# Splits and set loads of a Strassen-Winograd step pipeline moved between engines, stages and queues

## The chip, the cores and the metric

The kernel runs on one core of a Trainium2 chip. The metric is device microseconds of one execution; a time that is given as the kernel's is the median of several. The engines are TensorE (PE), VectorE (DVE), ScalarE (ACT), GpSimd (POOL) and SyncE (SP), which only issues DMAs here. Each engine works through its own instructions in order.

## What is computed

One pre-norm decoder layer on 1024 tokens and 16 meta tokens, model width 1024, MLP width 4096, all in float32:

```python
h = rms_norm(x, norm1_w)
(rq, rk, rv, rg, dq, dk, dv, cb, cc, cx, gates) = [h @ w_in[:, s:e] for s, e in column_bounds()]
ret  = head_layer_norm(retention(rq, rk, rv)) * silu(rg)
diff = diff_attention(dq, dk, dv, lam, subln_w, lam_init)
conv = cb * short_conv(cc * cx, conv_w)
g = sigmoid(gates)                                    # three gates per channel
merged = g[0] * (ret @ w_branch[0]) + g[1] * (diff @ w_branch[1]) + g[2] * (conv @ w_branch[2])
x = x + merged @ w_out
u = square(relu(rms_norm(x, norm2_w) @ w_up))
return rms_norm(x + u @ w_down, final_norm_w)         # meta tokens dropped
```

## The kernel before

**Products in two parts.** Each float32 operand of a large product is held as a high part (a rounding copy, made by ScalarE, sometimes VectorE) and a low part (operand minus high part, a subtraction on VectorE or GpSimd). A product is three matmuls: high with high, high with low, low with high. `split` does both parts; `lo_part` the second alone, on the engine that `pick` takes in turn from a list.

**Mixers and gates stage.** Up to about 1085 us the input projections, attention, retention and convolution run, ordered by a planner. The three branch results lie in DRAM (`cT`, `dT`, `rT`). Then comes the gates stage: 24 groups of gate columns, 48 matmuls each. `weights` loads two halves of a weight tile and splits them, the low parts on GpSimd. From the third group on `branch_sums(br, k)` forms the right operands of the later products for one branch and one block row: it loads four blocks, makes the sums T1 to T4 on VectorE and stores these four (`TD`). It runs twelve times. At group 14 the first four operands of the first branch are loaded and split (`SET`).

**Steps.** From 1349 us on the order is written by hand (`tc.manual_schedule()`). All products (three branches, output projection, up, down) are a list of steps. A `Quad` makes two output pairs by seven products each (Strassen-Winograd, one level); step i is product i for both pairs, p = 0 and 1, 24 matmuls (12 in the half-height down block). The right operands are B11, B21, T1, B22, T2, T3, T4 in this order (`ORDER`), the left ones are weight blocks and their sums. In iteration s the loop issues, in this order:

```python
steps[s - 1][3](1)          # evac of pair 1 of the step before
soon ; steps[s + 2][1]()    # prep: weight sums, high and low parts of step s + 2
steps[s][2](0) ; mid ; steps[s][2](1) ; steps[s][3](0)     # 24 matmuls; evac of pair 0
work ; fetch                # splits of the next right operands; loads and stores
steps[s + 3][0]()           # weight loads of step s + 3
```

`Quad.pe` takes a bank for product 1 (kept and added to in products 5 to 7) and one for products 2, or 3 and 4; there are 8 banks (`acc_bank`). `Quad.evac` copies a bank out (L859) or calls `use`: in the branches L934 to L940 (add, times gate, plus the merged sum), in up L1116 to L1123 (square of relu), in down L1169 and L1170 (add the residual). Rings of buffers: 10 weight blocks (`raw`), 5 tiles of both parts (`w`), 3 gate blocks (`g`), 16 blocks (`X`).

**Right operands.** Two sets of 14 buffers hold the seven operands of a branch or down block in two parts. `turn_over` replaces them during the last quad: the block is loaded whole into the low half's buffer (L899) and split in place by `build`. Up's operands are made from the normalised output projection (`up_t1`, `plain_op`, `up_sum`): a scaling or a subtraction per block, then its parts. The quads of up begin with products 1 and 2 of two quads, as the others need the second half of the tokens, whose scale `token_scale(1)` makes in up's first step. `up_use` forms the sums for down and stores them (`UD`).

Of the kernel before, what the change touches and what calls it, by code (L numbers as in the profile page):

```python
# [18 lines left out]
P = 128  # L19
# [52 lines left out]
def trunk_kernel(ctx: ExitStack, tc, x, w_in, w_branch, w_out, w_up, w_down, w_down2, w_down3, vecs, lam_in, consts, y):  # L72
# [643 lines left out]
    TD = {br: {n: dram([P, 4, 512]) for n in ORDER if n not in PLAIN} for br, _ in BR}  # L716

    def right_src(br, name):
        if name in PLAIN:
            z, j = PLAIN[name]  # L720
            return dict(BR)[br][:, 4 * z:4 * z + 4, half(j)]
        return TD[br][name]
# [20 lines left out]
    for n, (br, f) in enumerate((br, f) for br, _ in BR for f in range(KT)):  # L743
        wt = weights(w_in[G_GATE + br * KT + f])
# [8 lines left out]
        if n == 14:  # L753

            SET = {}
            for name in ORDER[:4]:
                oh, ol = opnd(True, [P, 4, 512]), opnd(True, [P, 4, 512])
                nc.sync.dma_start(out=f32(ol), in_=right_src(2, name))
                for k in range(4):
                    split(f32(ol[:, k]), oh[:, k], ol[:, k], v if k % 2 else nc.gpsimd)  # L760
                SET[name] = (oh, ol)
# [22 lines left out]
    count = {}  # L784

    def pick(key, engines):
        count[key] = count.get(key, -1) + 1
        return engines[count[key] % len(engines)]

    G = nc.gpsimd  # L790

    def lo_part(key, engines, src, hi, lo):
        pick(key, engines).tensor_tensor(out=lo, in0=src, in1=f32(hi), op=ALU.subtract)  # L793

    class Quad:


        def __init__(self, srcs, nk, B, use, lo_engines, pre=False):
            self.srcs, self.nk, self.B, self.use, self.pre = srcs, nk, B, use, pre
            self.lo_engines = lo_engines  # L800
            self.A = [[None, None] for _ in range(7)]
            self.raw = {}
            self.kept = {}
# [71 lines left out]
    def new_set(first):  # L875
        return {}

# [8 lines left out]
    def build(src, oh, ol, key="set"):  # L886
        e = pick(key + "c", (a, a, a, v))
        if e is a:
            a.copy(out=oh, in_=src)  # L889
        else:  # L890
            v.tensor_copy(out=oh, in_=src)  # L891
        lo_part(key + "l", (v, v, v, G), src, oh, ol)

    def turn_over(L, B, nk, source, left_names):

        for i, name in enumerate(ORDER):
            def load(name=name):
                open_op(B, name, nk, name in left_names)
                nc.sync.dma_start(out=f32(B[name][1]), in_=source(name))  # L899

            def split_op(name=name):
                oh, ol = B[name]
                for k in range(nk):
                    build(f32(ol[:, k]), oh[:, k], ol[:, k])

            at(fetch, L + i + 1, load)
            at(work, L + i + 3, split_op)
# [10 lines left out]
    WLO = (G, G, G, v)  # L918
    SETS = {2: SET, 1: {}, 0: {}}
    for n, (br, _) in enumerate(BR):  # L920
        for quad in range(2):
# [8 lines left out]
            def use(p, r, j, pt, sb, br=br, quad=quad, gt=gt):  # L930
# [13 lines left out]
            q = Quad(pairs_of(w_branch[br * KT:(br + 1) * KT], quad), 4, SETS[br], use, WLO)  # L944
            for i in range(7):
                product_step(q, i)
        if n < 2:
            nxt = BR[n + 1][0]
            turn_over(L, SETS[nxt], 4, lambda name, nxt=nxt: right_src(nxt, name), FIRST)


    for i, name in enumerate(ORDER[4:]):
        def load(name=name):
            open_op(SET, name, 4, False)
            nc.sync.dma_start(out=f32(SET[name][1]), in_=right_src(2, name))

        def split_op(name=name):
            for k in range(4):
                build(f32(SET[name][1][:, k]), SET[name][0][:, k], SET[name][1][:, k])

        at(fetch, -1, load)
        at(work, 2 + i, split_op)
# [5 lines left out]
    def merged(f, js):  # L968
        if f not in MO:
            MO[f] = opnd(True, [P, 2, SEQ])  # L970
        for j in js:
            build(M[f, j], MO[f][:, 0, half(j)], MO[f][:, 1, half(j)])
# [13 lines left out]
    class Out:  # L986
# [13 lines left out]
        def prep(self):  # L1000
            for z in range(2):
                w = temp("w", [P, 2, 512], F32R)
                a.copy(out=w[:, 0], in_=self.raw[z])
                lo_part("o", (G, v), self.raw[z], w[:, 0], w[:, 1])
# [13 lines left out]
        def evac(self, p):  # L1018
# [8 lines left out]
            else:  # L1027
                sq[j] = temp("t", [P, 512])
                a.activation(out=sq[j], in_=xc, func=AF.Square)
                if f < KT - 1:  # L1030
                    G.tensor_tensor(out=acc[j], in0=acc[j], in1=sq[j], op=ALU.add)

        def store(self):
            nc.sync.dma_start(out=xd[:, self.f, half(self.j)], in_=X2[self.f, self.j])
# [27 lines left out]
    def up_op(name, k, src):  # L1062
        if k == 0:
            open_op(US, name, 4, name in U_LEFT)
        build(src, US[name][0][:, k], US[name][1][:, k], "up")
# [34 lines left out]
    UD = [{name: dram([P, n, 512]) for name in ORDER} for _, n in BLOCKS]  # L1100
# [4 lines left out]
    def up_use(pair):  # L1105
        U = {}

        def put(dst, src):
            at(fetch, now[0] + 1, lambda: nc.sync.dma_start(out=dst, in_=src))

        def store(name, src):
            for b, (p0, n) in enumerate(BLOCKS):
                if p0 <= pair < p0 + n:
                    put(UD[b][name][:, pair - p0, :], src)
# [226 lines left out]
```

## Time and profile before

| | |
|---|---|
| median of 3 runs | 2460.97 us (2460.46 to 2461.25) |
| profiled execution, its own time | 2457.13 us |
| its span | 2455.3 us |
| mean granted TensorE clock | 0.979 |

The profile is of one execution. Times in it are us from the start of the span. Matmuls are pipelined, so one is recorded at about 0.39 us while they follow each other every 0.23 us; what a stretch gets done is read from the count of its matmuls. "Granted clock" is the share of 2.4 GHz that TensorE got: 1.00, or 0.50 (1.2 GHz). A releaser behind "<-" is what ended the idle time or the wait before an instruction.

### The profile page before, as it was taken

The page shows a single profiled execution, that of the slowest core. Times are in us where ns is not written, and L with a number is a line of the kernel's source. Part 1 is how long each engine was busy: PE and PEld are TensorE (multiplying, and loading weights), DVE is VectorE, ACT ScalarE, POOL GpSimd, SP SyncE. Part 2 cuts the span into 40 slices and gives each one's busy share as a digit, 9 for nine tenths or more (in the row PEclk, how much of TensorE's full clock was granted, in tenths as well). Part 3 has the DMA queues.
Part 4 walks back from the last instruction along what each step waited for, and adds up shares of the span by engine and source line. Part 5 has one row for each costly group of instructions (what it writes and reads, how often), then busy time and mean ns, then how long its engine had stood idle before and what let it go on. Part 6 is the DMA issues. An engine that isn't in the chain of part 4 may idle for free. (4 is left out here: it accounts for less than half of the span.)

```text
span 2455.3 us, 32724 instructions
## 1 busy us (share of the span) xinstructions
PE 2330.6 (95%) x11854; PEld 2009.7 (82%) x11854; DVE 1570.2 (64%) x2963; ACT 987.6 (40%) x1929; POOL 918.4 (37%) x804
## 2 busy tenths in 40 slices
PE   7999999999999999999999888789979999999997
PEld 7999999999999989987887676567758888777766
DVE  6776776776764676565511576764676767665666
ACT  5554554554543333333322342323333334443344
POOL 2132223233222212126632345444534434555564
PEclk9999999999999999999999999899989999999999
DMA  3111111111111111129822453325425446544132
GB/s 135 35 52 44 44 52 44 44 52 44 44 53 44 52 52 52 52 99 346 315 99 96 145 179 132 138 95 183 148 75 166 154 146 234 199 152 161 67 130 70
DMA packets 123139, 271.48 MB, mean 111 GB/s; under 512 B 13920, under 2 KB 18144, under 8 KB 118752
## 3 DMA queue, kind: packets, MB, share of 16 engines
q1 hardware_dynamic: 111840, 231.63, 27.6%
q0 software_dynamic: 11136, 37.76, 3.9%
q8 instruction: 93, 1.52, 0.3%
q14 instruction: 70, 0.57, 0.1%
HBM read 195.41 MB, written 73.92 MB: 110 GB/s over the span
## 5 line engine op out<-in xcount | busy, mean ns | idle before, releaser
L161 PE MATMUL pmm<-H,whi 128*128 128x512 f32 (+3 forms) x1640 | 574.3, 352 | 14.2 <-ACT H L196 8.5
L162 PE MATMUL pmm<-H,whi 128*128 128x512 f32 (+3 forms) x1640 | 574.0, 351 | 1.6 <-DVE H L197 1.5
L163 PE MATMUL pmm<-H,wlo 128*128 128x512 f32 (+3 forms) x1640 | 572.9, 350 | 0.0
L850 PE MATMUL pb<-op,w 128*128 128x512 f32 x1176 | 480.1, 408 | 89.0 <-DVE t L934 31.7
L136 POOL TENSOR_TENSOR wlo<-raw,whi 128x512 fp32r<-128x512 f32 x190 | 256.7, 1352 | 638.1 <-ACT whi L135 590.1
L793 POOL TENSOR_TENSOR w<-raw,w 128x512 fp32r<-128x512 f32 (+1 forms) x248 | 347.9, 1411 | 361.7 <-ACT w L820 339.7
L852 PE MATMUL pb<-op,w 128*128 128x512 f32 x1176 | 473.3, 403 | 2.9 <-POOL w L793 2.8
L851 PE MATMUL pb<-op,w 128*128 128x512 f32 x1176 | 473.3, 402 | 1.2 <-POOL op L793 1.2
L820 ACT CAST w<-raw 128x512 fp32r<-128x512 f32 (+1 forms) x308 | 181.9, 601 | 502.7 <-DVE raw L826 218.8
L850 PEld LDWEIGHTS pb<-op,w 128*128 128x128 f32 x1176 | 228.6, 194 | 156.6 <-ACT t L859 36.7
L161 PEld LDWEIGHTS pmm<-H,whi 128*128 128x128 f32 x1640 | 309.2, 189 | 40.5 <-ACT H L196 8.5
L162 PEld LDWEIGHTS pmm<-H,whi 128*128 128x128 f32 x1640 | 309.9, 189 | 27.0 <-DVE H L197 2.3
L163 PEld LDWEIGHTS pmm<-H,wlo 128*128 128x128 f32 x1640 | 309.7, 189 | 24.4
L852 PEld LDWEIGHTS pb<-op,w 128*128 128x128 f32 x1176 | 228.3, 194 | 58.2 <-POOL w L793 5.1
L851 PEld LDWEIGHTS pb<-op,w 128*128 128x128 f32 x1176 | 229.0, 195 | 52.5 <-POOL op L793 1.5
L135 ACT CAST whi<-raw 128x512 fp32r<-128x512 f32 x192 | 118.6, 619 | 193.6 <-PE pmm L162 70.7
L793 DVE TENSOR_TENSOR w<-raw,w 128x512 fp32r<-128x512 f32 (+1 forms) x92 | 87.2, 948 | 138.7 <-ACT w L820 98.2
L826 DVE TENSOR_TENSOR raw<-raw,raw 128x512 f32<-128x512 f32 (+1 forms) x176 | 130.9, 771 | 59.3 <-DMA raw<-w_branch 38.2
L793 DVE TENSOR_TENSOR op<-op,op 128x512 fp32r<-128x512 f32 x114 | 101.4, 941 | 30.9 <-ACT op L889 30.9
L859 ACT COPY t<-pb 128x512 f32<-128x512 f32 x132 | 75.8, 582 | 44.1 <-PE pb L852 43.8
L378 ACT ACTIVATE B<-B,nb 128x144 f32<-128x144 f32 (+3 forms) x64 | 50.6, 791 | 99.3 <-DVE nb L377 99.0
L793 POOL TENSOR_TENSOR op<-op,op 128x512 fp32r<-128x512 f32 x38 | 56.2, 1480 | 88.9 <-DVE op L891 79.6
(285 smaller groups left out, 3874.9 us busy)
## 6 DMA issues: line engine op xcount, KB each, us to landing
raw<-w_in SPq DMA_DIRECT2D x192, 256.0 KB, 2.6
op<-d SPq DMA_DIRECT2D x42, 1024.0 KB, 7.6
d<-X SPq DMA_DIRECT2D x118, 256.0 KB, 3.1
raw<-w_up SPq DMA_DIRECT2D x72, 256.0 KB, 4.4
raw<-w_down SPq DMA_DIRECT2D x56, 256.0 KB, 3.5
d<-t POOLq DMA_DIRECT2D x48, 256.0 KB, 3.8
raw<-d SPq DMA_DIRECT2D x48, 256.0 KB, 7.4
d<-raw POOLq DMA_DIRECT2D x48, 256.0 KB, 6.7
```

Source lines behind the costliest of these rows:

```text
L135: a.copy(out=hi, in_=src)
L136: (eng or v).tensor_tensor(out=lo, in0=src, in1=f32(hi), op=ALU.subtract)
L161: nc.tensor.matmul(pt, lhsT=hi[:, s], rhs=xh[:, c0:c0 + w], start=start, stop=False)
L162: nc.tensor.matmul(pt, lhsT=hi[:, s], rhs=xl[:, c0:c0 + w], start=False, stop=False)
L163: nc.tensor.matmul(pt, lhsT=lo[:, s], rhs=xh[:, c0:c0 + w], start=False, stop=stop)
L793: pick(key, engines).tensor_tensor(out=lo, in0=src, in1=f32(hi), op=ALU.subtract)
L820: a.copy(out=w[:, 0], in_=src)
L826: comb = lambda d, x0, x1, o: v.tensor_tensor(out=d, in0=x0, in1=x1, op=o)
L850: nc.tensor.matmul(pt, lhsT=w[0][:, s], rhs=b[0][:, k], start=first, stop=False, skip_group_check=True)
L851: nc.tensor.matmul(pt, lhsT=w[0][:, s], rhs=b[1][:, k], start=False, stop=False, skip_group_check=True)
L852: nc.tensor.matmul(pt, lhsT=w[1][:, s], rhs=b[0][:, k], start=False, stop=k == nk - 1, skip_group_check=True)
L859: a.copy(out=t, in_=pt)
```

## The change

In the steps GpSimd makes no additions or subtractions any more: low parts, additions of the merged sum, of the squares and of the residual all run on VectorE, high parts all on ScalarE. In the gates stage the weights' low parts go to VectorE too. `branch_sums` splits five of the seven operands (B11, B21, T1, B22, T2) and stores both parts; T3 and T4 stay whole. Set loads, the stores of the residual and of up's results go from SyncE's queue to GpSimd's. In up, B11 and B21 for down are split before they are stored; the sums of the second pair come a step later; relu and square run on ScalarE alone. Three quads of up, not two, lead with their first two products. In an iteration `work` comes before the evacuation of pair 0, and the weight loads before `fetch`.

```diff
+    READY = ORDER[:5]
+    TD = {br: {n: dram([P, 2, 4, 512] if n in READY else [P, 4, 512]) for n in ORDER} for br, _ in BR}
+    def ready(br, k, n, src):
+        w = temp("w", [P, 2, 512], F32R)
+        split(src, w[:, 0], w[:, 1])
+        nc.gpsimd.dma_start(out=TD[br][n][:, :, k], in_=f32(w))
...
+        for n, zj in PLAIN.items():
+            ready(br, k, n, b[zj])
...
-        for n, t in (("T1", t1), ("T3", t3), ("T2", t2), ("T4", t4)):
+        for n, t in (("T3", t3), ("T4", t4)):
             nc.gpsimd.dma_start(out=TD[br][n][:, k], in_=t)
+        ready(br, k, "T1", t1)
+        ready(br, k, "T2", t2)
...
-        wt = weights(w_in[G_GATE + br * KT + f])
+        wt = weights(w_in[G_GATE + br * KT + f], lo_eng=v)
...
-                oh, ol = opnd(True, [P, 4, 512]), opnd(True, [P, 4, 512])
-                nc.sync.dma_start(out=f32(ol), in_=right_src(2, name))
-                for k in range(4):
-                    split(f32(ol[:, k]), oh[:, k], ol[:, k], v if k % 2 else nc.gpsimd)
+                SET[name] = [opnd(True, [P, 4, 512]) for _ in range(2)]
+                for z in range(2):
+                    nc.sync.dma_start(out=f32(SET[name][z]), in_=TD[2][name][:, z])
...
-            a.copy(out=w[:, 0], in_=src)
-            lo_part("w", self.lo_engines, src, w[:, 0], w[:, 1])
+            split(src, w[:, 0], w[:, 1])
...
+    def turn_over(L, B, nk, source, in_parts, left_names):
+        def load(name, z):
+            if z == 0:
+                open_op(B, name, nk, name in left_names)
+            G.dma_start(out=f32(B[name][z]), in_=source(name)[:, z])
...
+            if name in in_parts:
+                for z in range(2):
+                    at(fetch, L + i + 1 + z, lambda name=name, z=z: load(name, z))
+            else:
+                at(fetch, L + i + 1, lambda name=name: whole_load(name))
+                whole += [(name, k) for k in range(nk)]
...
+        n0 = 7 - len(whole) // nk
+        for n, (name, k) in enumerate(whole):
+            at(work, L + n0 + 3 + n // 3 * (1 if nk == 4 else 2), lambda name=name, k=k: split_op(name, k))
...
-                    pick("m", (G, v)).tensor_tensor(out=M[f, j], in0=M[f, j], in1=g, op=ALU.add)
+                    v.tensor_tensor(out=M[f, j], in0=M[f, j], in1=g, op=ALU.add)
...
+    U_READY = ("B11", "B21")
+    UD = [{name: dram([P, 2, n, 512] if name in U_READY else [P, n, 512]) for name in ORDER} for _, n in BLOCKS]
...
-            if sb is None:
-                a.activation(out=u, in_=pt, func=AF.Relu)
-                a.activation(out=u, in_=u, func=AF.Square)
-            else:
+            if sb is not None:
                 v.tensor_tensor(out=u, in0=pt, in1=sb, op=ALU.add)
-                v.scalar_tensor_tensor(out=u, in0=u, scalar=0.0, in1=u, op0=ALU.max, op1=ALU.mult)
+            a.activation(out=u, in_=pt if sb is None else u, func=AF.Relu)
+            a.activation(out=u, in_=u, func=AF.Square)
...
-                at(work, now[0] + 1, sums)
+                at(work, now[0] + 1 + p, sums)
...
+            for name in U_READY:
+                u, h = U[PLAIN[name]], temp("X", [P, 512])
+                split(u, h.bitcast(F32R), u.bitcast(F32R))
+                store(name, h, u)
...
-    for q, i in [(q, i) for q in range(2) for i in range(2)] + [(q, i) for q in range(2) for i in range(2, 7)] + \
-            [(q, i) for q in range(2, 8) for i in range(7)]:
+    for q, i in [(q, i) for q in range(3) for i in range(2)] + [(q, i) for q in range(3) for i in range(2, 7)] + \
+            [(q, i) for q in range(3, 8) for i in range(7)]:
...
-            pick("d", (G, v)).tensor_tensor(out=sb, in0=sb, in1=xc, op=ALU.add)
+            v.tensor_tensor(out=sb, in0=sb, in1=xc, op=ALU.add)
...
                 steps[s][2](1)
-                steps[s][3](0)
             for fn in work.get(s, ()):
                 fn()
+            if 0 <= s < N:
+                steps[s][3](0)
+            if 0 <= s + LL < N:
+                steps[s + LL][0]()
             for fn in fetch.get(s, ()):
                 fn()
-            if 0 <= s + LL < N:
-                steps[s + LL][0]()
```

The same edits are made in the output projection (`Out.prep`, `Out.evac`, `Out.store`), in `up_op`, `merged`, `last_u`, `last_w` and in the loads of the first branch's T2, T3 and T4.

## Rows read from the trace of the kernel before

**Rows 1.** The page, part 1: busy us, share of the span, instructions.

```profile
PE 2330.6 (95%) x11854; PEld 2009.7 (82%) x11854; DVE 1570.2 (64%) x2963; ACT 987.6 (40%) x1929; POOL 918.4 (37%) x804
```

**Rows 2.** Windows: length, busy us (instructions) per engine, granted clock, DMA share, GB/s.

```profile
1097.00:1217.00 120.00, 118.48 (x511) 95.59 (x511) 68.72 (x78) 35.75 (x62) 75.72 (x99) 1.00 0.95 339
1217.00:1349.00 132.00, 131.75 (x571) 106.75 (x569) 18.92 (x25) 28.96 (x47) 43.79 (x49) 1.00 0.30 99
1349.00:1655.00 306.00, 255.93 (x1010) 201.29 (x1011) 206.90 (x245) 99.37 (x179) 142.87 (x96) 0.92 0.40 139
1655.00:1748.00 93.00, 90.42 (x387) 72.88 (x386) 47.12 (x58) 34.36 (x59) 43.49 (x32) 0.98 0.55 176
1748.00:1826.00 78.00, 57.49 (x204) 42.94 (x203) 58.73 (x79) 25.65 (x44) 29.98 (x21) 0.87 0.26 89
1826.00:2085.00 259.00, 259.00 (x1123) 211.44 (x1123) 177.77 (x219) 99.78 (x171) 103.84 (x72) 0.99 0.52 171
2085.00:2348.00 263.00, 245.29 (x1035) 196.53 (x1034) 167.01 (x223) 102.99 (x188) 145.84 (x105) 0.98 0.42 153
2348.00:2381.00 33.00, 28.18 (x116) 21.11 (x115) 23.71 (x40) 15.40 (x36) 21.72 (x21) 1.00 0.25 80
```

**Rows 3.** Waits of PE from 1349 to 2381: us in total, times, longest.

```profile
PE pb L850 <- DVE t L934: 31.7, 7, 5.3
PE pb L850 <- ACT t L859: 29.5, 12, 6.3
PE pb L850 <- DVE X L1170: 16.6, 8, 4.0
...
PE pb L1047 <- ACT t L1029: 0.2, 1, 0.2
```

**Rows 4.** Windows of one wait in the branches and the matmuls behind it.

```profile
1388.30:1392.90 4.60, 0.24 (x2) 0.00 (x0) 4.56 (x6) 0.99 (x2) 2.94 (x2) 0.90 0.18 57
1393.00:1398.60 5.60, 5.60 (x13) 4.40 (x14) 2.04 (x4) 0.62 (x1) 0.62 (x1) 0.50 0.56 185
```

**Rows 5.** Timeline of DVE: start, us, instruction, count merged.

```profile
1156.76 0.69 DVE L735 TENSOR_TENSOR raw<-raw,raw 128x512 f32<-128x512 f32 x1
...
1374.10 1.88 DVE L793 TENSOR_TENSOR op<-op,op 128x512 fp32r<-128x512 f32 x3
...
1384.32 4.07 DVE L793 TENSOR_TENSOR op<-op,op 128x512 fp32r<-128x512 f32 x3
```

**Rows 6.** Timeline of POOL at the first and the last of these.

```profile
1157.02 0.56 POOL L738 DMA_DIRECT2D d<-raw  x1 [0.94 <-DVE raw L734]
...
1383.81 3.44 POOL L793 TENSOR_TENSOR w<-raw,w 128x512 fp32r<-128x512 f32 x2
```

**Rows 7.** Groups of POOL from 1349 to 2381, the costliest: count | busy, mean ns.

```profile
L793 POOL TENSOR_TENSOR w<-raw,w 128x512 fp32r<-128x512 f32 x223 | 325.6, 1468 | 353.9 <-ACT w L820 332.1 <-ACT w L1003 21.4
```

**Rows 8.** Waits of SP's DMA queue from 1349 to 1655.

```profile
SPq L928 <- POOL X L940: 143.1, 13, 18.5
```

**Rows 9.** Groups of ACT from 1349 to 2381, the costliest.

```profile
L820 ACT CAST w<-raw 128x512 fp32r<-128x512 f32 x276 | 168.6, 620 | 470.8 <-DVE raw L826 205.2 <-PE pb L852 129.3 <-DMA raw<-w_branch 72.4
```

**Rows 10.** Timeline of DVE in the start of up.

```profile
1756.48 0.69 DVE L192 SCALAR_TENSOR_TENSOR k<-t,k 128x512 f32<-128x512 f32 x1
...
1813.82 0.68 DVE L1082 TENSOR_TENSOR X<-X,X 128x512 f32<-128x512 f32 x1
1815.18 0.69 DVE L793 TENSOR_TENSOR op<-X,op 128x512 fp32r<-128x512 f32 x1 [0.69 <-ACT op L889]
1815.79 0.68 DVE L1082 TENSOR_TENSOR X<-X,X 128x512 f32<-128x512 f32 x1
```

**Rows 11.** Window in the branches with the densest set loads.

```profile
1431.00:1443.00 12.00, 7.18 (x29) 5.51 (x28) 8.37 (x12) 4.04 (x8) 5.78 (x5) 0.87 1.03 387
```

**Rows 12.** Timeline of PE at token scale, in up's first step.

```profile
1751.22 1.02 PE L1046 MATMUL pb<-k,onesr 128*128 128x512 f32 x2
...
1753.04 0.80 PE L850 MATMUL pb<-op,w 128*128 128x512 f32 x1
```

More of the change, by code (lines that the diff above doesn't have):

```diff
@@ L782, in at, with __init__ @@
         table.setdefault(s, []).append(fn)
[L784 to L793, printed above, removed]
     class Quad:
-        def __init__(self, srcs, nk, B, use, lo_engines, pre=False):
+        def __init__(self, srcs, nk, B, use, pre=False):
             self.srcs, self.nk, self.B, self.use, self.pre = srcs, nk, B, use, pre
-            self.lo_engines = lo_engines
             self.A = [[None, None] for _ in range(7)]
@@ L884, in open_op, with whole_load, split_op @@
             B[name] = (both[:, 0], both[:, 1])
[L886 to L889, printed above, removed]
-        else:
-            v.tensor_copy(out=oh, in_=src)
-        lo_part(key + "l", (v, v, v, G), src, oh, ol)
-    def turn_over(L, B, nk, source, left_names):
-        for i, name in enumerate(ORDER):
[L897 to L907, printed above, removed]
+    G = nc.gpsimd
+    def turn_over(L, B, nk, source, in_parts, left_names):
[3 more added lines that the diff above has]
+            G.dma_start(out=f32(B[name][z]), in_=source(name)[:, z])
+        whole = []
+        for i, name in enumerate(ORDER):
+            if name in in_parts:
[4 more added lines that the diff above has]
+                whole += [(name, k) for k in range(nk)]
+        def whole_load(name):
+            open_op(B, name, nk, name in left_names)
+            G.dma_start(out=f32(B[name][1]), in_=source(name))
+        def split_op(name, k):
+            oh, ol = B[name]
+            split(f32(ol[:, k]), oh[:, k], ol[:, k])
+        n0 = 7 - len(whole) // nk
+        for n, (name, k) in enumerate(whole):
+            at(work, L + n0 + 3 + n // 3 * (1 if nk == 4 else 2), lambda name=name, k=k: split_op(name, k))
     def product_step(q, i):
@@ L948, in trunk_kernel, with last_load, last_split @@
             nxt = BR[n + 1][0]
-            turn_over(L, SETS[nxt], 4, lambda name, nxt=nxt: right_src(nxt, name), FIRST)
-    for i, name in enumerate(ORDER[4:]):
[L953 to L962, printed above, removed]
+            turn_over(L, SETS[nxt], 4, lambda name, nxt=nxt: TD[nxt][name], READY, FIRST)
+    def last_load(name):
+        open_op(SET, name, 4, False)
+        if name in READY:
+            for z in range(2):
+                G.dma_start(out=f32(SET[name][z]), in_=TD[2][name][:, z])
+        else:
+            G.dma_start(out=f32(SET[name][1]), in_=TD[2][name])
+    def last_split(name):
+        oh, ol = SET[name]
+        for k in range(4):
+            split(f32(ol[:, k]), oh[:, k], ol[:, k])
+    for i, name in enumerate(ORDER[4:]):
+        at(fetch, i, lambda name=name: last_load(name))
+        if name not in READY:
+            at(work, 2 + i, lambda name=name: last_split(name))
     MO = {}
@@ L971, in merged @@
         for j in js:
-            build(M[f, j], MO[f][:, 0, half(j)], MO[f][:, 1, half(j)])
+            split(M[f, j], MO[f][:, 0, half(j)], MO[f][:, 1, half(j)])
     for s, todo in ((3, ((0, (0, 1)), (1, (0, 1)))), (4, ((2, (0, 1)), (3, (0, 1)))), (5, ((4, (0,)), (6, (0,)))),
@@ L1002, in prep @@
                 w = temp("w", [P, 2, 512], F32R)
-                a.copy(out=w[:, 0], in_=self.raw[z])
-                lo_part("o", (G, v), self.raw[z], w[:, 0], w[:, 1])
+                split(self.raw[z], w[:, 0], w[:, 1])
                 self.w.append(w)
@@ L1030, in evac @@
                 if f < KT - 1:
-                    G.tensor_tensor(out=acc[j], in0=acc[j], in1=sq[j], op=ALU.add)
+                    v.tensor_tensor(out=acc[j], in0=acc[j], in1=sq[j], op=ALU.add)
         def store(self):
-            nc.sync.dma_start(out=xd[:, self.f, half(self.j)], in_=X2[self.f, self.j])
+            G.dma_start(out=xd[:, self.f, half(self.j)], in_=X2[self.f, self.j])
     for j in range(2):
@@ L1126, in use @@
                 return
-            for name, zj in PLAIN.items():
-                if zj == (r, j):
-                    store(name, u)
+            if (r, j) == (1, 1):
+                store("B22", u)
             if (r, j) == (1, 0):
-                at(work, now[0] + 1, sums)
+                at(work, now[0] + 1 + p, sums)
         def sums():
@@ L1187, in last_u @@
         both = opnd(True, [P, 2, SEQ])
-        nc.sync.dma_start(out=f32(both[:, 1]), in_=UL[j])
+        G.dma_start(out=f32(both[:, 1]), in_=UL[j])
         us.append((both[:, 0], both[:, 1]))
@@ L1192, in last_u_split @@
         for i in range(2):
-            build(f32(us[j][1][:, half(i)]), us[j][0][:, half(i)], us[j][1][:, half(i)])
+            split(f32(us[j][1][:, half(i)]), us[j][0][:, half(i)], us[j][1][:, half(i)])
     def last_w(fp):
@@ L1200, in last_w @@
             nc.sync.dma_start(out=raw, in_=w_down3[fp][:, z * HW:(z + 1) * HW])
-            a.copy(out=w[:, z, 0], in_=raw)
-            lo_part("w", WLO, raw, w[:, z, 0], w[:, z, 1])
+            split(raw, w[:, z, 0], w[:, z, 1])
             pair.append((w[:, z, 0], w[:, z, 1]))
```

32 lines of the change are left out of this document (12 added, 20 removed).

## Prediction

> **What bounds the kernel now.** I read the page first: TensorE is busy 95% of the span, VectorE and GpSimd far less [rows 1]. So the time can only come out of the stretches in which TensorE waits or runs slowly. The windows by stage show them [rows 2]. From 1826 to 2085 the steps run clean: 1123 matmuls in 259.0 us, 0.2306 us each, 5.53 us for a step of 24. At that price the other windows lose:
> - branch products 1349 to 1655: 306 - 1010 x 0.2306 = 73.1 us
> - output projection 1655 to 1748: 93 - 387 x 0.2306 = 3.8 us
> - start of up 1748 to 1826: 78 - 204 x 0.2306 = 31.0 us
> - end of up and down 2085 to 2348: 263 - 1035 x 0.2306 = 24.3 us
> - the half-height down block 2348 to 2381: 33 - 116 x 0.2306 = 6.3 us
>
> Together 138.5 us; from 1097 to 1349 TensorE hardly waits [rows 2]. The table of waits says who ends them [rows 3]: nearly all are evacuations of a PSUM bank on VectorE (L934, L1170) or ScalarE (L859). The eleven rows of that table, 31.7 to 0.2 us, add to 95 us; the other 43 us are the clock. After the wait of 4.4 us at 1388 the granted clock was 0.50, the 1.2 GHz level, and 13 matmuls took 5.6 us where a clean step has 24 [rows 4].
>
> Why is VectorE late? Three subtractions in a row take 1.88 us with GpSimd quiet, and 4.07 us while GpSimd subtracts beside them [rows 5]; GpSimd's own two then take 3.44 us [rows 6]. So one operation costs VectorE 0.63 us alone and up to 1.36 us beside GpSimd, and moving a GpSimd operation to VectorE costs 0.63 us and can give back as much or more. The Trainium skill, SBUF — State Buffer, section "SBUF: two separate sides", says the two share one port pair by an exclusive lock, against a VectorE operation with two SBUF inputs. The rows agree. A second cause is SyncE: its in-order queue stood 143 us behind gate loads that wait for GpSimd's additions to free their buffers [rows 8], and weight loads queue behind those; ScalarE's casts waited 72.4 us for weights [rows 9].
>
> **The change, part by part.**
> *Arithmetic off GpSimd.* In the steps 223 subtractions at full width [rows 7] and about 100 smaller groups go to VectorE. VectorE operations per seven steps (38.7 us): branch 8 combinations, 14 low parts, 22 evacuations, 8 splits = 52, 32.8 us; down 8 + 14 + 14 + 10 = 46, 29 us; up 8 + 14 + 6 + 12 = 40, 25 us. All fit, so the contention losses go where the order allows.
>
> *The order in a step.* Work now stands ahead of the evacuation of the first half. The second low part can't start before half a step, because the w ring has 5 tiles and ScalarE's cast waits for TensorE to free one [rows 9]: it ends at about 4.0 us. Then the step's splits, then the evacuation. TensorE needs that evacuation by 5.53 us only between products 3 and 4 and 5 and 6 (a copy on ScalarE) and between 6 and 7 (VectorE), which accumulate on a bank just read. With three splits in the step, VectorE's reader ends at 4.0 + 3 x 0.63 + 2 x 0.63 = 7.2 us, 1.6 us late. That is so once in each of three down quads, and less in the last up quad: 6 us, with 2 us for clock and small waits 8 us. In the branches splits stand in early steps: 0.25 us per quad, 1.5 us in all; the last quad carries 4, 4 and 2 splits of the merged sums: 3 us. Bounds for both together: 5 us (no wait beyond the seven counted) to 20 us (the 24.3 us of today nearly unchanged).
>
> *Loads.* Weight loads are issued ahead of the gate loads of a step, and sets go by GpSimd's queue, so the second cause goes. But a set in parts is 12 loads of 1 MB, not 7: 12.6 MB, with 4.2 MB of weights and 2.1 MB of gates in 38.7 us. At the best rate of this stretch, 387 GB/s [rows 11], that is 49 us. T3 and T4 come last and are split one or two steps into the next branch, about when they land: I take 2 us at each of two turns, 4 us; bounds 0 and 25 us (each load 10 us late at both turns, with the clock).
>
> *Start of up.* This is where I expect little. Each derived block is subtract, cast on ScalarE, low part: 1.97 us per block, 0.69 us of it VectorE waiting, and that without GpSimd [rows 10]; the change leaves this order. R2 is ready at 1757.2 [rows 10], 9 us after up begins. Then VectorE has, in order up to the evacuation of the sixth step: T1 4 x 2.6, B22 8 x 0.63, T2 and T3 8 x 1.97, ten low parts, six combinations and six evacuations at 0.63, and 5 us (my estimate) for casts that stand behind squares: 9 + 50 = 59 us. Three leading pairs hold 6 of the 8 banks for their second accumulator and 2 for the first, so the seventh step can't take a bank before that evacuation: TensorE could start it at 1.8 + 6 x 5.53 = 35 us (1.8 us is token scale, 1751.22 to 1753.04 [rows 12]), and waits 24 us. The copy after the seventh step stands behind T4's casts, another 5 us. With token scale and 2 us for the clock the stretch loses 33 us, as now 31. Bounds: 10 us (T4 alone 8 us late for its step) and 40 us.
>
> *Gates stage.* The step of making five parts per sum moves here: 60 splits, 0.62 us on ScalarE [rows 9] and 0.63 on VectorE each, and 48 weight low parts from GpSimd to VectorE. Per gate group (11 us) VectorE has 13 operations, 8.2 us, and ScalarE 9, 5.6 us: hidden behind TensorE. The DMA is what is short. Today 12 sums move 1 MB in and 1 MB out each, and the stretch 1097 to 1217 stands at DMA share 0.95, 339 GB/s [rows 2]; afterwards 3 MB go out, and the first set is 8 loads of 1 MB, not 4: 50.3 + 8.4 = 58.7 MB beside a steady 99 GB/s of weights and gates [rows 2]. At 339 - 99 = 240 GB/s that is 245 us, and from 1097 to 1349 there are 252. It just fits if it is spread out, and weights' low parts on VectorE now stand behind waits for DMAs. I take 8 us; bounds 0 and 125 us (below).
>
> *Rest.* The out stage keeps 2.5 us (token scale is TensorE's own work), the clean part of up gets 1.5 us of waits from two more splits a pair, the half-height block, whose steps are half as long against evacuations and splits of full width, keeps most of its 6.3: 5 us. Mixers and tail are untouched.
>
> **The sum.** Losses after: 1.5 + 3 + 4 branches, 2.5 out, 33 start of up, 1.5 up, 8 down, 5 half-height: 58.5 of 138.5, so 80 us gained; 8 us given back in the gates stage: 72 us. The profiled run took 2457.1 us, so 2385; the median stands 3.8 us above it: 2389 us.
>
> **Rivals.**
> - *The third pair pays* (0.12): the start of up loses 10, not 33 us: 2366 us. For it: six steps of lead instead of four. Against: the bank count and 1.97 us per block above.
> - *The gates stage becomes DMA-paced: slower* (0.07). One mechanism: the order of VectorE and ScalarE is fixed beforehand; if the 12 sums stay as dense in it as now (ended by 1217), everything queued behind them waits until 58.7 MB have moved, 1097 + 245 = 1342, and the 132 us of gate groups that now run from 1217 to 1349 come after it: 125 us, 2389 - 8 + 125 = 2506 us. It decides from about 80 us of gate work behind the last sum, seven groups. Against: today the sums are spaced as the DMA delivers, without a wait on TensorE. A part of it, 40 us, has 0.10: 2421 us.
> - *Sets arrive late* (0.10): T3 and T4 at the upper bound, 25 us instead of 4, with some weights late: 2412 us.
> - *GpSimd goes on disturbing VectorE* by writing the descriptors of its DMAs (0.05): half of the 80 us stays lost, 2429 us. Against: beside a GpSimd DMA issue of 0.56 us at 1157.02 [rows 6] a VectorE subtraction at 1156.76 took 0.69 us [rows 5]. The Trainium skill, SBUF — State Buffer, "SBUF: two separate sides", warns of the reverse: a VectorE operation that uses both ports for one tensor, such as a float32 copy, keeps GpSimd from writing descriptors, and its DMAs starve. By that rule the moved sets would wait only beside such copies, and the change takes L891, the copy of the steps, away; no run here shows more yet.
>
> **How the numbers follow.** The forecast has 0.56, from 2370 (gates 0; loads 4, down 3 and start of up 4 us less) to 2418 (gates 20, loads 14, start of up 40). Reaching from 2352, below the third pair's 2366, to 2440, above the 2429 of a disturbed VectorE, leaves out the DMA-paced case, a fifth of the three milder rivals and tails of the forecast: 0.17. A measurement of this kernel tells 0.2% (5 us) from no change. Faster: the forecast, the third pair and four fifths of the milder rivals, 0.88; of the last fifth 0.04 ends level; the rest with the DMA-paced case is slower, 0.08.
>
> **What would show it.** Right: L793, L826 and L939 on VectorE at 0.6 to 0.7 us; no L934 wait of 3 to 5 us from 1349 on and granted clock 1.00 in the branches; SyncE no longer behind gate loads; up's start still near 78 us, ended by VectorE or ScalarE; DMA share above 0.9 from 1097 to after 1300. Wrong: waits on whi or wlo in the gates stage above 10 us, waits for op<-d in the branches, or a start of up under 60 us.

## Result, and the profile after

The changed kernel takes 2419.8 us (median of 4 runs, 2416.7 to 2421.5) against 2460.7 (4 runs): a ratio of 0.983, 95% interval 0.982 to 0.985. It is faster by 41 us. The forecast was faster by 72 us, 2389 us. The profiled execution took 2421.53 us, its span is 2419.7 us; the two profiled spans lie 35.6 us apart, and the stages below add up to that. The time lies 2 us above the forecast's own range (2370 to 2418) and inside the wider one (2352 to 2440).

The page, part 1 (busy us, share of the span, instructions), against [rows 1]: GpSimd's busy time is halved, VectorE's hardly grows although it has 313 instructions more.

```profile
PE 2315.2 (96%) x11854; PEld 2001.1 (83%) x11854; DVE 1604.9 (66%) x3276; ACT 1070.8 (44%) x2079; POOL 483.4 (20%) x643
```

Windows at the changed kernel's own stages: gates, branches, out, start of up, rest of up, full down blocks, half-height block and tail. Columns as in [rows 2].

```profile
1097.00:1360.00 263.00, 254.80 (x1080) 205.50 (x1078) 131.84 (x204) 87.21 (x153) 78.70 (x129) 0.98 0.84 320
1360.00:1609.00 249.00, 238.85 (x1009) 191.86 (x1010) 180.49 (x279) 88.13 (x155) 15.51 (x29) 0.98 0.58 215
1609.00:1698.00 89.00, 89.00 (x390) 72.96 (x389) 56.73 (x88) 36.92 (x63) 8.12 (x15) 1.00 0.64 210
1698.00:1772.00 74.00, 46.18 (x172) 35.42 (x170) 47.39 (x73) 32.34 (x56) 0.54 (x1) 0.82 0.12 42
1772.00:2066.00 294.00, 277.96 (x1178) 222.44 (x1179) 182.88 (x287) 162.36 (x284) 75.36 (x141) 0.99 0.55 195
2066.00:2306.00 240.00, 234.26 (x1010) 188.45 (x1009) 173.60 (x275) 101.81 (x183) 16.73 (x32) 1.00 0.49 182
2306.00:2420.00 114.00, 92.21 (x468) 75.67 (x466) 78.71 (x149) 53.29 (x113) 23.25 (x20) 0.90 0.21 74
```

At the clean price of 0.2306 us a matmul the branches now lose 249 - 1009 x 0.2306 = 16.3 us (73.1 before), out nothing, the start of up 34.3, the rest of up 22.4, the full down blocks 7.1. Waits of TensorE from 1350 to 2380 (us in total, times, longest), against [rows 3]:

```profile
PE pb L840 <- ACT t L849: 24.9, 15, 6.3
PE pb L840 <- DVE X L1122: 22.8, 9, 16.3
PE pb L840 <- DVE X L1174: 8.3, 4, 3.1
PE pb L840 <- DVE g L1122: 5.7, 1, 5.7
PE pb L840 <- DVE t L927: 1.8, 1, 1.8
```

The branches' VectorE evacuation (L927, formerly L934) has gone from 31.7 us to 1.8. Most of what is left is up's: L1122 is its evacuation on VectorE (28.5 us), L849 a bank copy on ScalarE (15.3 of its 24.9 us in up).

Stage lengths in us, from the first matmul of a stage to the first of the next in each profiled execution ("rest" is the half-height block and the tail). The kernels on the right are the experiments below.

| stage | before | after | e1 | e3 | e10 | e13 | e12 |
|---|---|---|---|---|---|---|---|
| branches begin at | 1349.6 | 1360.1 | 1359.8 | 1346.9 | 1348.6 | 1348.4 | 1358.7 |
| branches | 305.1 | 248.7 | 241.9 | 283.8 | 245.9 | 246.8 | 237.0 |
| out | 93.7 | 88.8 | 88.9 | 94.5 | 88.8 | 88.9 | 88.8 |
| up | 345.9 | 368.1 | 351.0 | 341.4 | 343.0 | 333.3 | 334.2 |
| full down | 253.7 | 239.9 | 235.7 | 239.1 | 239.1 | 239.1 | 236.6 |
| rest | 107.3 | 114.1 | 112.2 | 107.7 | 108.1 | 108.0 | 108.0 |
| span | 2455.3 | 2419.7 | 2389.5 | 2413.4 | 2373.5 | 2364.5 | 2363.3 |

So the branches give 56.4 us, full down 13.8 and out 4.9; the gates take back 10.5, up 22.2 and the rest 6.8.

### The profile page after: what moved, and what is told of

The parts are those of the page before. It is cut to its first block, busy times and chain, and to the rows that moved or that the text cites. A ratio compares the mean times of both kernels' runs of the same rounds, so it can differ in the third digit from the quotient of the medians.

```text
span 2419.7 us, 32940 instructions
## 1 busy us (share of the span) xinstructions
PE 2315.2 (96%) x11854; PEld 2001.1 (83%) x11854; DVE 1604.9 (66%) x3276; ACT 1070.8 (44%) x2079; POOL 483.4 (20%) x643
## 5 line engine op out<-in xcount | busy, mean ns | idle before, releaser
L840 PE MATMUL pb<-op,w 128*128 128x512 f32 x1176 | 472.7, 402 | 64.9 <-ACT t L849 24.9
L842 PE MATMUL pb<-op,w 128*128 128x512 f32 x1176 | 466.9, 397 | 0.0
L841 PE MATMUL pb<-op,w 128*128 128x512 f32 x1176 | 466.7, 397 | 0.0
L136 DVE TENSOR_TENSOR w<-raw,w 128x512 fp32r<-128x512 f32 (+1 forms) x400 | 263.8, 670 | 250.3 <-ACT w L135 246.8
L135 ACT CAST w<-raw 128x512 fp32r<-128x512 f32 (+1 forms) x400 | 237.2, 603 | 395.5 <-PE pb L842 195.1
L840 PEld LDWEIGHTS pb<-op,w 128*128 128x128 f32 x1176 | 224.5, 191 | 130.6 <-ACT t L849 32.3
L136 POOL TENSOR_TENSOR wlo<-raw,whi 128x512 fp32r<-128x512 f32 x142 | 192.8, 1359 | 594.0 <-ACT whi L135 539.6
L842 PEld LDWEIGHTS pb<-op,w 128*128 128x128 f32 x1176 | 224.3, 191 | 52.5 <-DVE w L136 0.9
L841 PEld LDWEIGHTS pb<-op,w 128*128 128x128 f32 x1176 | 224.8, 191 | 49.8 <-issue 0.2
L1108 POOL DMA_DIRECT2D d<-X x130 | 69.5, 540 | 284.4 <-ACT X L1124 163.5
L816 DVE TENSOR_TENSOR raw<-raw,raw 128x512 f32<-128x512 f32 (+1 forms) x176 | 111.5, 662 | 5.8 <-DMA raw<-w_branch 4.0
L849 ACT COPY t<-pb 128x512 f32<-128x512 f32 x132 | 74.5, 581 | 39.1 <-PE pb L842 39.0
L754 ACT ACTIVATE t<-t 128x512 f32<-128x512 f32 x48 | 30.3, 632 | 132.1 <-DVE t L250 132.1
L880 POOL DMA_DIRECT2D op<-d x36 | 19.3, 540 | 289.9 <-PE pb L842 287.8
```

The lines of the kernel that those rows point to most:

```text
L135: a.copy(out=hi, in_=src)
L136: (eng or v).tensor_tensor(out=lo, in0=src, in1=f32(hi), op=ALU.subtract)
L816: comb = lambda d, x0, x1, o: v.tensor_tensor(out=d, in0=x0, in1=x1, op=o)
L840: nc.tensor.matmul(pt, lhsT=w[0][:, s], rhs=b[0][:, k], start=first, stop=False, skip_group_check=True)
L841: nc.tensor.matmul(pt, lhsT=w[0][:, s], rhs=b[1][:, k], start=False, stop=False, skip_group_check=True)
L842: nc.tensor.matmul(pt, lhsT=w[1][:, s], rhs=b[0][:, k], start=False, stop=k == nk - 1, skip_group_check=True)
```

## The experiments

Times are medians of 4 runs (10 for e4), ratios are to the kernel before, measured anew beside each group of experiments (2458.5 to 2462.7 us). A difference of less than some 4 us between experiments of different groups says nothing.

### e1: evacuations ahead of the work again

```diff
                 steps[s][2](1)
+                steps[s][3](0)
             for fn in work.get(s, ()):
                 fn()
-            if 0 <= s < N:
-                steps[s][3](0)
```

> The changed kernel with one thing undone: in each step the evacuation of the first pair stands again ahead of the step's extra work (operand building, sums), as in the kernel before; all else stays changed. Theory A (what the change lost in up is that evacuations stand behind the extra work on ScalarE and VectorE, so that the seventh step waits 16.3 us for a bank, two later steps 4.0 us each and five quads 1.2 us): the loss of up falls from 58 us to about 30, the waits of TensorE that end on the ScalarE copies shrink, time 2385 to 2402. Rival B (the chain subtract, ScalarE cast, low part at 1.97 us a block sets the start of up, the order hardly matters): the wait moves to the operands and the time stays at 2412 to 2424.

2390.3 us, 0.971 (0.970 to 0.973), 29.5 us below the changed kernel. Theory A holds in the time, and less in up: of 30.2 us of span, up gives 17.1, the branches 6.8, full down 4.2, and up's loss (its length less 1344 matmuls at 0.2306 us) falls from 58 us to 41, not to 30. The changed kernel's VectorE timeline shows what the order did in the start of up (start, us, instruction, count, idle before):

```profile
1753.29 0.68 DVE L1080 TENSOR_TENSOR X<-X,X 128x512 f32<-128x512 f32 x1
1754.66 0.69 DVE L136 TENSOR_TENSOR op<-X,op 128x512 fp32r<-128x512 f32 x1 [0.69 <-ACT op L135]
1755.27 0.68 DVE L1080 TENSOR_TENSOR X<-X,X 128x512 f32<-128x512 f32 x1
1756.63 0.69 DVE L136 TENSOR_TENSOR op<-X,op 128x512 fp32r<-128x512 f32 x1 [0.69 <-ACT op L135]
1757.24 1.28 DVE L1122 TENSOR_TENSOR X<-pb,t 128x512 f32<-128x512 f32 x2
```

The two additions that free the banks come when the last block of the group is done, and TensorE's next matmul starts at once behind the first of them (its timeline):

```profile
1758.07 0.76 PE L840 MATMUL pb<-op,w 128*128 128x512 f32 x1 [16.31 <-DVE X L1122]
```

The same stands in up's ordinary steps, where the sums of a finished pair (L1135 on) go ahead:

```profile
1812.22 0.68 DVE L1135 TENSOR_TENSOR X<-X,X 128x512 f32<-128x512 f32 x1
...
1815.36 0.68 DVE L136 TENSOR_TENSOR X<-X,X 128x512 fp32r<-128x512 f32 x1
1815.96 0.68 DVE L1122 TENSOR_TENSOR X<-pb,t 128x512 f32<-128x512 f32 x1
```

And in the branches, at the third step behind a turn, ScalarE's bank copy stands behind three casts of a set; TensorE waits 3.4 us for it, and 1.9 in e1:

```profile
1456.58 1.65 ACT L135 CAST op<-op 128x512 fp32r<-128x512 f32 x3
1458.14 1.05 ACT L849 COPY t<-pb 128x512 f32<-128x512 f32 x2
```

But a wait of 11.5 us stays in e1's start of up, again ended by L1122. That part of rival B was true, and e6 is for it.

### e2: two leading quads instead of three

```diff
-pre=q < 3))
+pre=q < 2))
-for q, i in [(q, i) for q in range(3) for i in range(2)] + [(q, i) for q in range(3) for i in range(2, 7)] + ...
+for q, i in [(q, i) for q in range(2) for i in range(2)] + [(q, i) for q in range(2) for i in range(2, 7)] + ...
```

> The changed kernel with two leading quads in up instead of three. Theory A (the third leading quad finds no free bank, since the evacuations stand behind the work): the lead of two steps (11 us) is worth nothing, time 2412 to 2425, and the 16 us wait is replaced by a wait of like size for an operand. Rival C (the third quad does cover work that the operands need, only a size of the forecast is off): about 11 us slower, 2428 to 2436.

2416.1 us, 0.982 (0.980 to 0.983): not told from the changed kernel. In place of the wait of 16.3 us there is one of 18.2 us for a bank copy (L849), not for an operand. The third quad is worth nothing; rival C is out.

### e3: the engine alone, in the kernel before

```diff
-    WLO = (G, G, G, v)
+    WLO = (v,)
-        lo_part(key + "l", (v, v, v, G), src, oh, ol)
+        lo_part(key + "l", (v,), src, oh, ol)
-                    pick("m", (G, v)).tensor_tensor(out=M[f, j], ...)
+                    v.tensor_tensor(out=M[f, j], ...)
```

and likewise `pick("d", ...)`, the low parts of out, `acc` in out, the first set's low parts, and `lo_eng=v` for the gate weights.

> The kernel before with one part of the change alone: all GpSimd arithmetic of the steps, of the first set and of the gate weights' low parts goes to VectorE; the sets are still loaded whole on SyncE's queue and split in the steps, two leading quads, the order in a step as before. Theory (VectorE's slow subtractions beside GpSimd, 1.3 to 1.8 us instead of 0.63, made the branches' loss of 73 us): the loss of the branches falls below 30 us, time 2410 to 2435. Rival (VectorE, which now has the set builds and everything else, becomes the bound; the split sets were needed): waits on VectorE return, time 2450 to 2480.

2418.0 us, 0.983 (0.981 to 0.984): the whole net gain of the change with this one part. Full down gives 14.6 us, up 4.5, but the branches only 21.3; they still lose 51 us, so half of what the theory expected of them. VectorE's groups in the branches say why. Before (1349 to 1655) low parts and combinations took 0.82 to 1.11 us:

```profile
L793 DVE TENSOR_TENSOR op<-op,op 128x512 fp32r<-128x512 f32 x51 | 48.6, 1005 | 15.3 <-ACT op L889 15.3
L826 DVE TENSOR_TENSOR raw<-raw,raw 128x512 f32<-128x512 f32 x48 | 38.1, 817 | 40.1 <-DMA raw<-w_branch 38.2 <-POOL w L793 1.4
L793 DVE TENSOR_TENSOR w<-raw,w 128x512 fp32r<-128x512 f32 x21 | 23.4, 1113 | 23.7 <-ACT w L820 22.7 <-ACT w L1003 1.0
```

In e3 (1347 to 1631) they take 0.69 us, but VectorE waits for raw weights nearly as long as before (34.7 us, 38.2).

```profile
L793 DVE TENSOR_TENSOR op<-op,op 128x512 fp32r<-128x512 f32 x68 | 43.9, 688 | 1.2 <-ACT op L889 0.6
L826 DVE TENSOR_TENSOR raw<-raw,raw 128x512 f32<-128x512 f32 x48 | 31.8, 688 | 35.2 <-DMA raw<-w_branch 34.7
```

SyncE's queue in the same window still stands behind gate loads, now for VectorE's additions:

```profile
SPq L928 <- DVE X L940: 153.4, 27, 15.0
SPq L928 <- DVE X L937: 71.3, 13, 14.1
```

### e4: three of four weight low parts back on GpSimd

```diff
-            split(src, w[:, 0], w[:, 1])
+            WN[0] += 1
+            split(src, w[:, 0], w[:, 1], v if WN[0] % 4 == 3 else nc.gpsimd)
```

> The changed kernel with three of four low parts of the weights in the product steps back on GpSimd, as in the kernel before; all else stays changed. Theory (contention of GpSimd arithmetic with VectorE): VectorE's 512-column subtractions go from 0.66 to 1.0 us or more on the mean, the losses in the branches and in up grow, time 2440 to 2500. Rival (the gain came from the split sets and the queues, not from the engine): VectorE has slack now, time 2412 to 2428.

2460.1 us, 0.999 (0.998 to 1.000): 40 us slower than the changed kernel, the whole gain gone, with sets, queues and order as changed. Branches 257.4 us, up 382.4, full down 252.3. Groups of GpSimd and VectorE from 1359 to 2404:

```profile
L136 POOL TENSOR_TENSOR w<-raw,w 128x512 fp32r<-128x512 f32 x206 | 287.5, 1402 | 464.3 <-ACT w L135 439.6 <-DMA raw<-w_up 9.5 <-DMA g<-d 5.8
...
L136 DVE TENSOR_TENSOR w<-raw,w 128x512 fp32r<-128x512 f32 x101 | 81.7, 813 | 211.2 <-ACT w L135 210.9
L136 DVE TENSOR_TENSOR op<-op,op 128x512 fp32r<-128x512 f32 x84 | 64.9, 824 | 20.6 <-ACT op L135 20.6
```

The last of them takes 684 ns in the changed kernel. VectorE's slowing was smaller than the 1.0 us that the theory named; GpSimd works 206 times here and not 223 plus the sets. A low part also takes GpSimd itself 1402 ns, against VectorE's 690 in the changed kernel. How the 40 us divide between the two was not tried.

### e6: subtractions in groups, with e1's order

```diff
         for k in range(4):
             v.tensor_tensor(out=blk(*dst, k), in0=blk(*x0, k), in1=blk(*x1, k), op=ALU.subtract)
+        for k in range(4):
             up_op(name, k, blk(*dst, k))
```

and the same in `up_t1`, on top of e1.

> The kernel of e1_order_back, and in the operands of up that are differences all subtractions of a group come first and then its casts and low parts, so that VectorE no longer waits 0.69 us in every block for ScalarE's cast. Theory (with the order back, VectorE's own queue sets the start of up: its bank-freeing addition stands behind four blocks of 1.98 us): 14 to 16 waits of 0.69 us go, 8 to 11 us less than e1's 2390, so 2378 to 2384. Rival (the wait of 11.5 us that e1 shows is one of banks alone, and VectorE would have been in time): 2387 to 2393.

2375.7 us, 0.966 (0.964 to 0.967): 14.6 us below e1, more than expected. The start of up is 53.3 us (from the first matmul of up to that of the eighth step; e1 64.4, changed kernel 74.9). VectorE's timeline has four blocks in 4.8 us:

```profile
1726.18 2.49 DVE L1081 TENSOR_TENSOR X<-X,X 128x512 f32<-128x512 f32 x4
1728.59 2.49 DVE L136 TENSOR_TENSOR op<-X,op 128x512 fp32r<-128x512 f32 x4
```

where e1 took 7.9 us for the same four, with 0.69 us of idle time ahead of each low part. So with the order back VectorE's queue did set the start of up.

### e7 and e8: two leading quads with e1's order, and with e6's

The diff is that of e2, on top of e1 and of e6.

> The kernel of e1_order_back with two leading quads in up instead of three. Theory (the third quad pays once evacuations come first): two steps of lead are lost, 5 to 11 us slower than e1's 2390, so 2395 to 2401. Rival (the third quad's first two products hold the last free banks and only add VectorE work while the operands are made): no slower than e1, 2384 to 2391.

> Both: evacuations first, subtractions in groups, two leading quads. If the third quad pays, 5 to 11 us slower than e6_order_batched; if it brings nothing, within 4 us of it or faster.

e7 2389.0 us, 0.971 (0.970 to 0.973); e8 2377.1 us, 0.966 (0.965 to 0.968): each within 1.4 us of its kernel with three. The third quad pays in no order of the step.

### e9: set loads on SyncE's queue

```diff
-            G.dma_start(out=f32(B[name][z]), in_=source(name)[:, z])
+            nc.sync.dma_start(out=f32(B[name][z]), in_=source(name)[:, z])
```

in `turn_over` and `last_load`, for whole loads too; stores stay on GpSimd's queue.

> The changed kernel with the loads of the right operands back on SyncE's queue, behind the weights' loads of their step; all else stays changed (evacuations behind the work too). Theory (a second cause beside GpSimd's arithmetic: on SyncE's queue the set loads, which wait for a buffer, hold up the weights, as in e3_only_engine, where the branches still lost 51 us with VectorE 35 us in wait for raw weights): the branches lose 16 us more or above, time 2430 to 2455. Rival (what e3 lacked is that the sets come in two parts, with no casts and low parts left in the steps; the queue is of no account): 2414 to 2425.

2412.1 us, 0.980 (0.978 to 0.982): not slower but 7.7 us faster than the changed kernel. My theory fell: GpSimd's queue is not what helped. The branches take 244.4 us (248.7), full down 243.2 (239.9), the rest 107.6 (114.1). Most of the rest's gain lies behind the last operation of VectorE. In the changed kernel that is (chain that ended last: start, us)

```profile
2409.07 1.87 DVE op L1267 x4
```

and the span ends 8.7 us behind it; in e9 it is

```profile
2406.26 1.87 DVE op L1267 x4
```

and the span ends 3.9 us behind it. The raw trace shows what stands there: GpSimd's closing drain instruction lasts 10.8 us in the changed kernel and ends 4.8 us after SyncE's, when all results have landed; in e9 it lasts 5.6 us and ends before SyncE's. So it is in every kernel here. Where GpSimd issues 374 DMAs (the changed kernel, e1, e2, e4, e6, e7, e8, e11) the drain lasts 10.8 to 10.9 us and the span ends 8.7 us behind the last operation; with 310 (e9, e12) it is 5.6 to 5.7 and 3.9; with 120 (before, e3, e10, e13) 2.9 and 3.7. What the drain waits for is not shown.

### e10: e3 and the weight loads first

```diff
+            if 0 <= s + LL < N:
+                steps[s + LL][0]()
             for fn in fetch.get(s, ()):
                 fn()
-            if 0 <= s + LL < N:
-                steps[s + LL][0]()
```

> The kernel of e3_only_engine (the kernel before with all GpSimd arithmetic of the steps on VectorE) with one more part of the change: weight loads are issued ahead of the gate and set loads of their step. Theory L (the branches' 51 us that e3 still lost come from weight loads that stand behind gate loads on SyncE's queue, so that VectorE waits 35 us for raw weights): the branches lose 15 to 25 us, time 2380 to 2395. Rival S (they come from the casts and low parts of whole sets in the steps, which only the sets in two parts take away): 2408 to 2420.

2375.1 us, 0.965 (0.963 to 0.966): 42.9 us below e3, and 44.7 below the changed kernel. Theory L holds, with more than it expected: the branches lose 13.4 us. VectorE's wait for raw weights, 34.7 us in e3, is 4.6, while SyncE's queue still stands 178 us behind gate loads:

```profile
L826 DVE TENSOR_TENSOR raw<-raw,raw 128x512 f32<-128x512 f32 x46 | 30.3, 687 | 5.0 <-DMA raw<-w_branch 4.6
```

```profile
SPq L928 <- DVE X L940: 123.8, 25, 13.9
SPq L928 <- DVE X L937: 54.0, 12, 14.6
```

The queue stands for a like share of the time (in e3 225 us in 284, here 178 in 246); what counts is that the weights are ahead of the gates in it. The changed kernel's queue stands there too (1350 to 1610):

```profile
SPq L921 <- DVE X L933: 125.9, 25, 16.3
SPq L921 <- DVE X L930: 74.1, 11, 23.7
```

And before (1349 to 1655) it stood behind VectorE's own additions beside the 143.1 us behind GpSimd's [rows 8]:

```profile
SPq L928 <- DVE X L937: 69.3, 13, 16.0
SPq L928 <- DVE X L940: 27.6, 8, 5.9
```

The sets are whole and split in the steps here, 68 low parts of 0.69 us in the branches, and yet the branches lose no more than the changed kernel's 16.3 us: Rival S is out as the main cause.

### e11: the first set later

```diff
-        if n == 14:
-            SET = {}
-            for name in ORDER[:4]:
+        if n == 14:
+            SET = {}
+        if n in (16, 18, 20, 22):
+            for name in ORDER[n // 2 - 8:n // 2 - 7]:
```

> The changed kernel with the first set's loads spread in the gates stage: one name of two 1 MB parts in each of the gate groups 16, 18, 20 and 22 instead of all eight loads at group 14. Theory (these 8 MB, issued between 1163 and 1190 into a DMA that moves 412 to 419 GB/s there, hold up the gate weights, and TensorE waits 7.5 us in two places and runs at half clock for 10): the two waits go, 8 to 11 us less, 2408 to 2413. Rival (the sums' stores in two parts are what fills the DMA there): waits of like size remain, 2416 to 2422.

2418.4 us, 0.982 (0.981 to 0.984): no difference, and no verdict, because in this stage instructions are put in order by their costs: the eight loads were issued from 1152 to 1174, where the changed kernel has them too (not from 1163 to 1190, as I wrote). The DMA view from 1160 to 1205 of the changed kernel (line, count, KB each, median us to landing) shows gate weights that land 18.7 us after their issue, in between the set loads:

```profile
DMA packets 5153, 18.76 MB, mean 417 GB/s; under 512 B 664, under 2 KB 664, under 8 KB 4234
...
op<-d SPq DMA_DIRECT2D x4, 1024.0 KB, 22.2
raw<-w_in SPq DMA_DIRECT2D x6, 256.0 KB, 18.7
```

and of e10, where the sums are stored once:

```profile
DMA packets 6521, 15.39 MB, mean 342 GB/s; under 512 B 933, under 2 KB 933, under 8 KB 6517
...
raw<-w_in SPq DMA_DIRECT2D x9, 256.0 KB, 5.4
```

The changed kernel's TensorE waits there in two places for casts of gate weights (1097 to 1360), and its granted clock is 0.91 from 1180 to 1200 and 0.83 from 1200 to 1220:

```profile
PE pmm L161 <- ACT whi L135: 5.0, 1, 5.0
PE pt L161 <- ACT whi L135: 2.5, 1, 2.5
```

e10 has no such wait and enters the branches 11.5 us earlier. Which must go, the stores, the 8 MB of the first set or the splits made here, is open.

### e12 and e13: the two best

e12 is the changed kernel with the edits of e1, e6, e9 and e11. e13 is e10 with the grouped subtractions of e6: no set in two parts, two leading quads, work after the evacuation, no GpSimd arithmetic in the steps, weight loads first.

> Changed kernel with evacuations first, subtractions in groups, sets on SyncE's queue and the first set spread over later gate groups. From e6's 2375.7: 4 to 8 us less for the queue (as e9 against the changed kernel), 8 to 11 us less for the gates: 2357 to 2364 if the parts add; 2367 to 2372 if one of them is worth nothing beside the others.

> The kernel of e10_engine_loads (the kernel before with all GpSimd arithmetic of the steps on VectorE and the weight loads ahead of the other loads of their step) with the subtractions of up's derived operands in groups ahead of their casts and low parts. Theory (VectorE's own queue sets the start of up in this order of a step too): the grouping gives here what it gave between e1 and e6, 12 to 16 us, time 2359 to 2364, which would also be below e12's 2365.2 without any set in two parts and without a third leading quad. Rival (at the start of up e10 waits for ScalarE's bank copies, 6.1, 5.1 and 6.2 us, which stand behind casts; grouping the casts puts more of them ahead of such a copy): 2372 to 2380.

e12 2365.2 us, 0.961 (0.960 to 0.962); e13 2366.5 us, 0.962 (0.960 to 0.964): the same within the intervals, 54 us below the changed kernel. e12 lies between the two ranges that I had for it, 10.4 us below e6; e11's edit moves no load in it either (1151 to 1173), so most of that is the sets' queue: between the profiled spans the branches give 5.7 us and the rest, with its shorter drain, 4.7. e13 fell short of 2364 at its start of up, where bank copies still wait (5.3, 2.5 and 3.2 us): grouping gave 8.6 us, not 12. e12's branches are 10 us shorter and begin 10 us later. The two differ in order and queue too, so what the sets in two parts give by themselves in the branches was not measured; on the whole e12, which has them, is no faster than e13 without.

## Why the forecast was right in sign and 31 us off

Stage by stage, forecast and measured change in the profiled spans: gates +8 and +10.5; branches -64.6 and -56.4; out -1.3 and -4.9; up and full down -12.8 and +8.4; rest -1.3 and +6.8. They sum to -72 and -35.6. That the time falls beside 2421 us, the price of a gates stage in part paced by DMA, is chance: that stage gave back 10.5 us and not 40.

- **Arithmetic off GpSimd: right.** e3 and e4 show it from both sides: 43 us won by it alone, 40 lost when the weight low parts go back. The Trainium skill, SBUF — State Buffer, section "SBUF: two separate sides", names the exclusive lock on a shared port pair; the durations agree with a conflict (0.69 us for VectorE's low parts without GpSimd arithmetic, 0.81 to 0.82 in e4, 1.0 to 1.1 in the branches before), and no row shows a lock as such.
- **Loads: the effect right, the reason half wrong.** I wrote that the second cause goes because weight loads stand ahead of gate loads and sets move to GpSimd's queue, and took as a sign that SyncE would no longer stand behind gate loads. It stands there still, 200 us from 1350 to 1610 (L921, for VectorE's L930 and L933); I had counted the 143 us behind GpSimd's additions alone, and 97 us behind VectorE's stood beside them (under e10). The order of the weight loads does it, 43 us (e10 against e3). The queue of the sets gave nothing: back on SyncE's they are 8 us faster (e9), 10 in e6's order of a step (e12 against e6).
- **The order in a step: the term that was mis-sized.** I priced work ahead of the evacuation where a product accumulates on a bank just read: 8 us in down and the last up quad, 1.5 us in the clean part of up. Full down came as said (7.1 us left), but the rest of up, with its last quad, lost 22.4 us. A pair of up has not only two more splits: its sums are six VectorE operations in one step, ahead of the evacuations. They stand in the prediction's count of VectorE's work (the 12 of up), but not in its price of the order. Undoing the order gave 29.5 us (e1): 17 in up, 7 in the branches, 4 in full down. That this is nearly the whole miss is in part chance, for it takes from stages that came as forecast too, and it is not all of up's: from up's fifteenth step to the first of down the loss is 19.8 us in the changed kernel, 10.1 in e1, 1.6 in e10 and 2.7 before. What the other half comes of (the splits of B11 and B21, the later sums, the squares on ScalarE: all in e1 and none in e10) no run takes apart.
- **Start of up: the mechanism right, the size a little low.** Forecast were 33 us, 34.3 measured (window 1698 to 1772), with the bank wait at the seventh step as foretold: 59 us after up begins, and it began after 60.4. For 24 us of wait there and 5 for the copy behind it, 5.7 ahead of the sixth step, 16.3 ahead of the seventh and 6.3 for the copy were measured. That window ends before the eighth step starts; the first 14 steps of up lose 38.3 us, 33.3 before. That I took its chain of 1.97 us a block as given hid the cheapest gain: grouping is worth 9 to 15 us (e13, e6).
- **Branches' turns:** 4 us forecast, for sets that land late. TensorE waits 7.9 us for bank copies (L849) in the branches, 3.4 and 3.5 us of it behind the third step after each turn; with sets on SyncE these two are 2.7 and 2.5 (e9). The copies stand behind the set's casts (under e1), so this is the order in a step again.
- **Gates: right** (8 and 10.5), and by DMA as said. Their rival of 125 us did not come.
- **Rest: missed**, 6.8 us that I had at -1.3: 5.0 of them lie behind the last matmul (14.3 us to the end of the span, 9.3 before), where the program waits for GpSimd's drain, long with the sets' loads on GpSimd's queue (e9). I took the tail as untouched. The wait of 3.1 us (L1174) in the half-height block is no part of it, as 3.1 us stood there before too (L1170).
- **Rivals.** The third quad pays: out (e2, e7, e8). Sets late: not seen; in the branches ScalarE waits once for a set's load, 3.4 us, and TensorE never. GpSimd disturbs by descriptors: out; VectorE's low parts take 690 ns both in e3, where GpSimd issues one DMA in the branches, and in the changed kernel, where it issues 29.

Put together, the forecast of 80 us gained less 8 given back is met, and exceeded, by two of the change's parts (e10, 2460.7 - 2375.1 = 85.6 us). All the others together cost 44.7 us, of which the order in a step is the largest (29.5 us), the gates stage with its doubled traffic, some 11 us, the second, and the sets' queue, 8 us, the third.

## What to carry to other kernels

Before work is put ahead of an evacuation, count every operation of every table that falls into that step, on each engine, and ask for each evacuation who takes its bank next; here a reorder of two lines cost 29.5 us inside a change that looked like a gain. An in-order DMA queue that had to block was cheap here once what the path needs stood ahead of what blocks. Undo a change of many parts one by one: two edits held all of its gain, and a regrouping of subtract, cast, subtract, which the change did not touch, gave more than its third quad.

## What was not expected of the hardware

The end of the program waits for GpSimd's closing drain, and that lasted 2.9 us in the kernels with 120 DMAs issued by GpSimd, 5.6 to 5.7 us with 310 and 10.8 to 10.9 us with 374; only the last of these held up the end, by 5 us. Gate weights of 256 KB landed in 5.4 us with 342 GB/s moving and in 18.7 us with 417 GB/s and 1 MB loads ahead of them on their queue: some 20% more traffic, more than three times the delay.
